# A two-layer decoder trunk: the gate columns of the MLP's up-projection by seven block products in every group

## The chip, the cores and the metric

One core of a Trainium2 chip runs the kernel as one program. TensorE (PE) multiplies matrices and writes its results to PSUM; its weight loads (PEld) overlap its matmuls. VectorE (DVE) and ScalarE (ACT) do elementwise work on SBUF and PSUM, GpSimd (POOL) a little of it on SBUF, and SyncE (SP) issues most DMAs. The metric is device time in microseconds; smaller is better.

## The reference

The input x is 512 tokens of 1024 features in f32. Two layers follow each other. Each is a mixer with an output projection (layer 0: sliding-window attention and a short convolution; layer 1: chunked gated linear attention, GLA), then a gated MLP, then a gated embedding. Every part adds to x. The MLP is what the change touches:

```python
def _rms_norm(x, gain):
    y = x * rsqrt(mean(x * x, axis=-1) + 1e-6)
    return y * gain

def _conv_ffn(h, w_up, conv_w, conv_b, w_down):       # h = _rms_norm(x, ffn_norm)
    u = causal_depthwise_conv(h @ w_up, conv_w) + conv_b       # 1024 -> 5632, width 3 along the tokens
    gate, up = split(u, 2, axis=-1)                            # 2816 each
    return (gelu(gate) * up) @ w_down                          # 2816 -> 1024
```

## The kernel before

**Layout and precision.** Activations lie transposed: x is eight tiles `xT[m]` of 128 features x 512 tokens. Every f32 operand is split into two parts of type fp32r, high and low (`split`, L97, for activations; `cut`, L119, and `cut_blocks`, L803, for weights): ACT copies the high part and DVE subtracts it from the operand to get the low one. A product is then three matmuls, high x high, high x low, low x high (`mm3`, L154; L863 to L865 for the block products). All of it fits into SBUF; weights come in loads of 1 MB by SP into two buffers `raw`, and their split parts go into three buffers `wh` and three `wl` of 1024 columns.

**Order.** The code is a straight program. A scheduler orders each engine's instructions by their place in the program and by when it expects them to be ready; each engine then runs its list strictly in that order. Inside `manual_schedule` TensorE's order is the program's own. A tile with a tag takes the next free buffer of that tag, and waits until one is free. The tags that matter here: `a0`, `a1`, `b0`, `b1` (eight tiles of 128x512 each), `four` (seven of 128x2048), `zt` (two), `z` (three), and in a small pool `sq` (two), `R` (two) and `acc` (one). PSUM has four banks `ps` and four `pa`.

**The norm.** In the output projection (`project`, L350) two blocks of output features at a time are multiplied: 8 input blocks x 3 matmuls of 512 columns for each. When a block is done, `residual` (L377) adds it to `xT[m]` (L379), and `advance` (L259) splits `xT[m]` times the gain (L105, L106) and sums the squares into `acc` (L270, L271). `end_norm` (L318) sums `acc` over the features with eight small matmuls (L324) and makes 1/rms of each token on DVE (L167) and POOL (L168); `spread` (L331) turns that into R, a tile that has each token's factor in every partition, with two matmuls (L345). The factor may be applied after a product, since it belongs to a token.

**The up-projection** (`ffn`, L894) has eleven groups d of two gate columns (128 features each) and two value columns. Groups 0 to 3 are plain: four columns of 24 matmuls with x that lacks R, and `taps` (L906) multiplies each result by R (L916) before the convolution (L917 on ACT, two L919 on DVE). While groups 0 and 1 run, `sums` (L775) makes x with gain and R (L782) and four sums and differences of its blocks and token halves, and splits them; in group 3 `normed` (L992) splits x with R again. Groups 4 to 10 (`SEVEN = (4, 11)`, L32) take their two gate columns from seven products of blocks instead of eight, the scheme of Winograd and Strassen: the weights' even and odd input blocks by two columns, x's even and odd blocks by two token halves. `seven` (L848) is a generator whose products run between the two value columns; `seven_forms` (L817) makes the weight blocks: plain, t13, t2, and later `last`. TensorE's order in such a group is: second value column, blocks 0 to 5 (`begin`, L1012); block product 1 of x's plain even blocks; the rest of that value column; product 2 with the sums s1; two products; half of the first value column; one product; the other half; two products. Results come out of `seven` without a product with R, since x has it; the second gate column needs one sum with the part `more` (L911).

**After the groups** the products gate x value are split for the down-projection (`split_acts`, L959, and `split_blocks`, L967) and `down` (L1099) works through a written plan of steps: rows B (f = 0 to 7), A (8 to 13), and C (14 to 21), C by seven block products for four or three of the four pairs of output blocks. In layer 1, `blocks` (L282) prepares the last norm's input, also by sums.

**The end of layer 1's mixer:** `gate` and `gated` (L1567, L1573) make the GLA's eight output blocks; the split results lie in tiles of the mixer's own pool until the projection has read them.

Of the kernel before, what the change touches and what calls it, by code (L numbers as in the profile page):

```python
# [9 lines left out]
F32 = mybir.dt.float32  # L10
# [21 lines left out]
SEVEN = (4, 11)  # L32
# [25 lines left out]
class Kernel:  # L58
# [223 lines left out]
    def blocks(self, m, gain, scratch):  # L282
# [4 lines left out]
        tags = ("a0", "a1") if m < 4 else ("b0", "b1")  # L287
# [62 lines left out]
    def project(self, load, ks, n_out, done, first=()):  # L350


        nk = len(ks)
        for m2 in range(0, n_out, 2):
            pss = [self.ps(), self.ps()]
            lead = [k0 for k0 in first if m2 == 0]
            k0s = lead + [k0 for k0 in range(0, nk, 8) if k0 not in lead]
            for k0 in k0s:
                kn = min(8, nk - k0)
                with self.tc.high_priority(offset=300 if lead else 0):  # L360
                    raw = self.raw(kn, 2 * P)
                    load(raw, k0, slice(m2 * P, (m2 + 2) * P))
                    w = self.cut(raw, "b")
                for c in range(2):
                    for k in range(kn):
                        self.mm3(
                            pss[c], w(k, c * P, (c + 1) * P), ks[k0 + k],
                            start=k0 == k0s[0] and k == 0, stop=k0 == k0s[-1] and k == kn - 1,
                        )
            for c in range(2):  # L370
                done(m2 + c, pss[c])

    def rows(self, w2d):
        wv = w2d.rearrange("(k p) n -> p k n", p=P)
        return lambda raw, k0, cols: self.nc.sync.dma_start(raw, wv[:, k0 : k0 + raw.shape[1], cols])

    def residual(self, gain):  # L377
        def done(m, ps):
            self.nc.vector.tensor_tensor(self.xT[m], self.xT[m], ps, ALU.add)  # L379
            self.advance(m, gain)  # L380

        return done
# [57 lines left out]
    def mixer0(self):  # L440
        nc, a, tc = self.nc, self.a, self.tc
        with tc.tile_pool(name="m0", bufs=1) as mp:
# [317 lines left out]
            self.begin_norm(("a0", "a1"))  # L760

            def load(raw, k0, cols):
                w = a["hy_w_out"][0]
                for g in range(2):
                    nc.sync.dma_start(
                        raw[64 * g : 64 * g + 64, :4, :],
                        w[256 * g : 256 * g + 256, cols].rearrange("(j p) n -> p j n", p=64),
                    )
                nc.sync.dma_start(raw[:, 4:, :], w[512:, cols].rearrange("(k p) n -> p k n", p=P))

            self.project(load, ya + yc, ND, self.residual(self.g_ffn[0]))
            self.end_norm()


    def sums(self, j, gain, R, scratch):  # L775


        nc = self.nc
        H = S // 2
        for u in range(2):  # L780
            m = 2 * j + u
            nc.vector.scalar_tensor_tensor(  # L782
                out=scratch[:, u], in0=self.xT[m], scalar=gain[:, m : m + 1], in1=R, op0=ALU.mult, op1=ALU.mult
            )
        e, o, s12, s34 = (scratch[:, u] for u in range(4))
        out = []
        nc.vector.tensor_tensor(s12[:, :H], e[:, H:], o[:, H:], ALU.add)
        nc.vector.tensor_tensor(s12[:, H:], s12[:, :H], e[:, :H], ALU.subtract)
        nc.vector.tensor_tensor(s34[:, :H], e[:, :H], e[:, H:], ALU.subtract)
        nc.vector.tensor_tensor(s34[:, H:], o[:, :H], s12[:, H:], ALU.subtract)  # L790
        for x in (s12, s34):
            hl = self.pair(self.fp, "b0", "b1")
            self.split(hl, x)
            for c in (slice(0, H), slice(H, S)):
                out.append((hl[0][:, c], hl[1][:, c]))
        return out
# [97 lines left out]
    def ffn(self, i, next_gain):  # L894
        nc, a, tc = self.nc, self.a, self.tc
        xg, R = self.xg, None
        gain = self.g_ffn[i]
        wu = a["ffn_w_up"][i].rearrange("(k p) n -> p k n", p=P)
        w0, w1, w2, bb = self.fcv
        with tc.tile_pool(name=f"ffn{i}", bufs=1) as fp:  # L900
            forms, kept, acts = [], [], [None] * NF
# [4 lines left out]
            def taps(y, ps, f, more=None, normed=True):  # L906
                z = ps
                if more is not None:
                    z = fp.tile([P, S + 2], F32, tag="z", name=self.nm("z"), bufs=3)[:, :S]
# [4 lines left out]
                elif not normed:  # L914
                    z = fp.tile([P, S + 2], F32, tag="z", name=self.nm("z"), bufs=3)[:, :S]
                    nc.vector.tensor_tensor(z, ps, R, ALU.mult)  # L916
# [7 lines left out]
            def columns(w, c, bank):  # L924
                ps = bank()
                for k in range(ND):
                    self.mm3(ps, w(k, c * P, (c + 1) * P), xg[k], start=k == 0, stop=k == ND - 1)
                return ps

            def loaded(d):  # L930
                out = [self.raw(ND, 256) for _ in range(2)]
                for raw, cols in zip(out, (gates(d), values(d))):
                    nc.sync.dma_start(raw, wu[:, :, cols])
                return out
# [1034 lines left out]
```

## Time and profile before

| What | Value |
|---|---|
| median of 3 runs | 1234.95 us (1234.46 to 1235.18) |
| the profiled execution, its own time | 1235.43 us |
| span of its profile | 1233.7 us |
| DMA traffic | 117.56 MB, mean 95 GB/s |
| output projection of layer 0 on TensorE | 140.6 to 184.3 us |
| plain groups 0 to 3 of layer 0 | 184.3 to 272.8 us |
| block groups 4 to 10 of layer 0 | 272.8 to 420.0 us |
| down-projection of layer 0 | 420.0 to 541.8 us |

The profile is one execution, recorded by the hardware; its times are counted from the span's start. A row of the page's groups gives line, engine, operation, output and inputs with their shapes, the count, then busy us and mean ns of one, then the idle time of the engine just before them and who ended it. A row of the timeline gives start, duration and the same names, and in brackets the idle time before it. "Busy" for TensorE counts a matmul to its modelled end, so consecutive matmuls overlap; the distance between two starts is what one costs.

### The profile page before, as it was taken

How to read it: one execution, taken by the hardware profiler on the slowest of the kernel's cores; microseconds unless marked ns; L12 is line 12 of the kernel's file. 1: busy time of each engine (PE TensorE's matmuls, PEld its weight loads, DVE VectorE, ACT ScalarE, POOL GpSimd, SP SyncE). 2: the span in 40 equal slices, each digit the busy share in tenths (PEclk: the TensorE clock that was granted, in tenths of full speed). 3: DMA queues.
4: the chain of work that ended last, by engine and by line, in shares of the span. 5: the costliest groups of instructions: out<-in, count | busy, mean ns of one | idle time of the engine just before them, and what ended most of it. 6: DMA issues, size and time to landing. Idle time of an engine off the chain costs nothing.

```text
span 1233.7 us, 16975 instructions
## 1 busy us (share of the span) xinstructions
PE 1222.7 (99%) x6740; PEld 1045.2 (85%) x6740; DVE 920.2 (75%) x1449; ACT 640.7 (52%) x1036; POOL 43.6 (4%) x64
## 2 busy tenths in 40 slices
PE   9999999999999999999999999999999999999998
PEld 8877788889999889888987888888889989889887
DVE  6886556987788986746679875558977779977595
ACT  7466434555556744534563554435455556645374
POOL 2500000000000000000100000000000000000000
PEclk9999999999999999999999999999999999999999
DMA  6221332323223333222322222322322322422501
GB/s 216 87 87 48 87 102 74 103 69 112 94 96 110 120 103 95 94 87 91 112 91 68 69 70 69 103 93 86 103 101 80 118 88 95 145 86 95 195 2 69
DMA packets 111060, 117.56 MB, mean 95 GB/s; under 512 B 2777, under 2 KB 106259, under 8 KB 110981
## 3 DMA queue, kind: packets, MB, share of 16 engines
q1 hardware_dynamic: 109616, 115.35, 28.7%
q8 instruction: 53, 0.87, 0.3%
q0 software_dynamic: 560, 0.42, 0.2%
q10 hardware_dynamic: 804, 0.70, 0.2%
q14 instruction: 27, 0.21, 0.1%
HBM read 114.37 MB, written 2.10 MB: 94 GB/s over the span
## 4 chain that ended last, share of the span: by engine, by line
PE 86%; DVE 9%; ACT 2%; issue 2%; POOL 1%; DMA 0%; ACTq 0%; DVEq 0%; POOLq 0%
PE ps L158 16%; PE ps L159 16%; PE ps L160 16%; PE pa L159 5%; PE pa L158 5%; PE pa L160 5%; PE ps L863 4%; PE ps L865 4%; PE ps L864 4%; PE pa L865 2%; PE pa L864 2%; PE pa L863 2%; DVE wl L139 1%; PE ps L1382 1%; PE ps L1381 1%
## 5 line engine op out<-in xcount | busy, mean ns | idle before, releaser
L138 ACT ACTIVATE wh<-raw 128x1024 fp32r<-128x1024 f32 (+4 forms) x170 | 169.4, 999 | 225.3 <-PE ps L159 168.0
L139 DVE TENSOR_TENSOR wl<-raw,wh 128x1024 fp32r<-128x1024 f32 (+4 forms) x170 | 195.1, 1149 | 95.1 <-ACT wh L138 94.8
L158 PE MATMUL ps<-a,wh 128*128 128x512 f32 x416 | 162.7, 391 | 0.0
L159 PE MATMUL ps<-a,wh 128*128 128x512 f32 x416 | 162.3, 390 | 0.0
L160 PE MATMUL ps<-a,wl 128*128 128x512 f32 x416 | 162.1, 390 | 0.0
L158 PE MATMUL ps<-b,wh 128*128 128x512 f32 x320 | 126.5, 396 | 0.6 <-ACT b L102 0.5
L160 PE MATMUL ps<-b,wl 128*128 128x512 f32 x320 | 125.7, 393 | 0.0
L159 PE MATMUL ps<-b,wh 128*128 128x512 f32 x320 | 125.2, 392 | 0.0
L811 ACT ACTIVATE wh<-raw 128x1024 fp32r<-128x1024 f32 x54 | 57.1, 1057 | 69.2 <-DVE raw L836 30.0
L158 PEld LDWEIGHTS ps<-a,wh 128*128 128x128 f32 x416 | 78.1, 188 | 16.6 <-issue 0.7
L159 PEld LDWEIGHTS ps<-a,wh 128*128 128x128 f32 x416 | 78.2, 188 | 16.4 <-issue 0.3
L160 PEld LDWEIGHTS ps<-a,wl 128*128 128x128 f32 x416 | 78.1, 188 | 16.3
L158 PE MATMUL pa<-a,wh 128*128 128x512 f32 x224 | 87.8, 392 | 0.0
L159 PE MATMUL pa<-a,wh 128*128 128x512 f32 x224 | 87.8, 392 | 0.0
L160 PE MATMUL pa<-a,wl 128*128 128x512 f32 x224 | 87.1, 389 | 0.0
L812 DVE TENSOR_TENSOR wl<-raw,wh 128x1024 fp32r<-128x1024 f32 x54 | 65.9, 1221 | 24.0 <-ACT wh L811 23.9
L158 PEld LDWEIGHTS ps<-b,wh 128*128 128x128 f32 x320 | 60.1, 188 | 13.9 <-ACT b L102 1.3
L919 DVE SCALAR_TENSOR_TENSOR zt<-z,vfa,zt 128x511 f32<-128x511 f32 (+1 forms) x92 | 67.2, 748 | 5.3 <-ACT zt L917 5.0
L160 PEld LDWEIGHTS ps<-b,wl 128*128 128x128 f32 x320 | 60.1, 188 | 12.8
L159 PEld LDWEIGHTS ps<-b,wh 128*128 128x128 f32 x320 | 60.2, 188 | 11.6
L160 PEld LDWEIGHTS pa<-a,wl 128*128 128x128 f32 x224 | 42.1, 188 | 9.2
L158 PEld LDWEIGHTS pa<-a,wh 128*128 128x128 f32 x224 | 42.3, 189 | 7.2
(460 smaller groups left out, 2942.4 us busy)
## 6 DMA issues: line engine op xcount, KB each, us to landing
raw<-in_ffn_w_up_dram SPq DMA_DIRECT2D x44, 1024.0 KB, 5.0
raw<-in_ffn_w_down_dram SPq DMA_DIRECT2D x13, 1024.0 KB, 5.1
raw<-in_hy_w_in_dram SPq DMA_DIRECT2D x8, 1024.0 KB, 5.0
raw<-in_gla_w_in_dram SPq DMA_DIRECT2D x8, 1024.0 KB, 5.2
raw<-in_ffn_w_down_dram SPq DMA_DIRECT2D x8, 768.0 KB, 4.6
raw<-in_ple_w_gate_dram SPq DMA_DIRECT2D x6, 1024.0 KB, 5.1
raw<-in_gla_w_out_dram SPq DMA_DIRECT2D x4, 1024.0 KB, 4.9
zt<-in_ffn_w_down_dram SPq DMA_DIRECT2D x6, 512.0 KB, 3.6
```

Of the source, the lines that this page charges most:

```text
L138: nc.scalar.activation(hv, v, AF.Copy)
L139: nc.vector.tensor_tensor(lv, v, hv.bitcast(F32), ALU.subtract)
L158: mm(out, lh, rh, start=start, stop=False, **kw)
L159: mm(out, lh, rl, start=False, stop=False, **kw)
L160: mm(out, ll, rh, start=False, stop=stop, **kw)
L811: nc.scalar.activation(h, src, AF.Copy)
L812: nc.vector.tensor_tensor(l, src, h.bitcast(F32), ALU.subtract)
L863: mm(out, wh, xh, start=first and j == 0, stop=False, **kw)
L864: mm(out, wh, xl, start=False, stop=False, **kw)
L865: mm(out, wl, xh, start=False, stop=j == ND // 2 - 1, **kw)
L919: nc.vector.scalar_tensor_tensor(out=y[:, tap:], in0=z[:, : S - tap], scalar=w[:, f : f + 1], in1=y[:, tap:], op0=ALU.mult, op1=ALU.add,)
L1381: mm(o, lh, rl, start=False, stop=False, **kw)
```

## The change

All eleven groups of both layers become block groups, and x enters them with its gain but without R.

- `sums`, `normed`, `residual` and the plain groups go. The projection now belongs to the MLP: the mixers return a function, and `ffn` calls it with `done`, which adds the residual and calls the new `operand(m)`. It copies `xT[m]` times the gain on ACT, splits the copy, and at each odd m makes and splits the four sums of that pair; then the square is summed. The sums' parts lie in four `four` buffers.
- `project` calls `then` ahead of the last two residuals; that is `prepare(0)`, which loads and cuts the weights of group 0.
- Group 0 contains `end_norm` after the first half of its first value column and `spread` after the second half.
- `taps` multiplies every result by R, the second gate column after its sum with `more`.
- `place` keeps the products of groups 0 to 3 in single tiles; `split_one` splits f = 0 to 5 in groups 4 to 9 and f = 6, 7 in the last; the double splits of f = 8, 10, 12 come after the groups, and the plan of `down` begins with B instead of A.
- The tags `a0`, `a1` and `b0`, `b1` change roles in layer 1 (`mine`, `other`), and the GLA's split results go to `a1`, `a0` and `R`, since the mixer's pool is closed before the projection.

```diff
-SEVEN = (4, 11)
-    def project(self, load, ks, n_out, done, first=()):
+    def project(self, load, ks, done, then):
+        for m2 in range(0, ND, 2):
             pss = [self.ps(), self.ps()]
+            raw = self.raw(ND, 2 * P)
+            load(raw, slice(m2 * P, (m2 + 2) * P))
+            w = self.cut(raw, "b")
+            for c in range(2):
+                for k in range(ND):
+                    self.mm3(pss[c], w(k, c * P, (c + 1) * P), ks[k], start=k == 0, stop=k == ND - 1)
+            if m2 + 2 == ND:
+                then()
             for c in range(2):
                 done(m2 + c, pss[c])
...
+    def operand(self, m, gain, tags):
+        nc, fp = self.nc, self.mlp
         H = S // 2
+        if m % 2 == 0:
+            self.scratch = self.four(fp, F32)
+        x = self.scratch[:, m % 2]
+        nc.scalar.activation(x, self.xT[m], AF.Copy, scale=gain[:, m : m + 1])
+        self.xg.append(self.pair(self.fp, *tags))
+        self.split(self.xg[m], x)
+        if m % 2:
+            e, o, s12, s34 = (self.scratch[:, u] for u in range(4))
+            nc.vector.tensor_tensor(s12[:, :H], e[:, H:], o[:, H:], ALU.add)
+            nc.vector.tensor_tensor(s12[:, H:], s12[:, :H], e[:, :H], ALU.subtract)
+            out = self.four(fp)
+            self.split((out[:, 0], out[:, 1]), s12)
+            nc.vector.tensor_tensor(s34[:, :H], e[:, :H], e[:, H:], ALU.subtract)
+            nc.vector.tensor_tensor(s34[:, H:], o[:, :H], s12[:, H:], ALU.subtract)
+            self.split((out[:, 2], out[:, 3]), s34)
+            self.forms.append([(out[:, q, c], out[:, q + 1, c]) for q in (0, 2) for c in (slice(0, H), slice(H, S))])
+        self.squares(m)
...
+        mine, other = (("a0", "a1"), ("b0", "b1"))[:: 1 - 2 * i]
...
-            def taps(y, ps, f, more=None, normed=True):
-                z = ps
-                if more is not None:
-                    z = fp.tile([P, S + 2], F32, tag="z", name=self.nm("z"), bufs=3)[:, :S]
+            def taps(y, ps, f, more=None):
+                z = fp.tile([P, S + 2], F32, tag="z", name=self.nm("z"), bufs=3)[:, :S]
+                if more is None:
+                    nc.vector.tensor_tensor(z, ps, R, ALU.mult)
+                else:
...
-                elif not normed:
-                    z = fp.tile([P, S + 2], F32, tag="z", name=self.nm("z"), bufs=3)[:, :S]
-                    nc.vector.tensor_tensor(z, ps, R, ALU.mult)
+                    nc.vector.tensor_tensor(z, z, R, ALU.mult)
...
+            def split_one(f):
+                tag = other[1 if f < 4 else 0]
+                h = self.fp.tile([P, S], F32R, tag=tag, name=self.nm("uh"))
+                pool, tag = (self.fp, tag) if f < 7 else (self.sp, "R")
+                acts[f] = h, pool.tile([P, S], F32R, tag=tag, name=self.nm("ul"))
+                self.split(acts[f], kept[f])
...
             def split_acts():
-                for f in (8, 10, 12):
-                    split_pair(f)
-                split_kept(0)
-                split_kept(1)
+                for f in (6, 7):
+                    split_one(f)
...
+            self.begin_norm(mine)
+            self.forms = []
+            xg = self.xg
+            ready = []
+            def done(m, ps):
+                nc.vector.tensor_tensor(self.xT[m], self.xT[m], ps, ALU.add)
+                self.operand(m, gain, mine)
+            project(done, lambda: ready.extend(prepare(0)))
+            steps, w1c, w0c = ready
+            with tc.manual_schedule(engines={ET.PE}):
+                late = begin(0, steps, w1c)
+                for d in range(groups):
+                    g, y = both(), both()
+                    next(steps)
+                    V0 = self.pa()
+                    value(w0c, V0, 0, ND // 2)
+                    if d == 0:
+                        self.end_norm()
+                    next(steps)
+                    value(w0c, V0, ND // 2, ND)
+                    if d == 0:
+                        R = self.spread()
+                    X, Y, more = next(steps)
+                    rest = late
+                    if d + 1 < groups:
+                        steps, w1c, w0c = prepare(d + 1)
+                        late = begin(d + 1, steps, w1c)
+                    else:
+                        split_acts()
+                    rest(y)
+                    taps(y[:, 0], V0, NF + 2 * d)
+                    taps(g[:, 0], X, 2 * d)
+                    taps(g[:, 1], Y, 2 * d + 1, more)
+                    nc.scalar.activation(g, g, AF.Gelu)
+                    place(d, g, y)
+                    if 4 <= d < groups - 1:
+                        split_one(d - 4)
...
+            for f in (8, 10, 12):
+                split_pair(f)
             self.down(i, acts, down_forms, both, work, finish)
...
-        plan = [(0, "A", 0, 3), (0, "A", 3, 6), (0, "B", 0, 4), (0, "B", 4, 8)]
+        plan = [(0, "B", 0, 4), (0, "B", 4, 8), (0, "A", 0, 3), (0, "A", 3, 6)]
...
             def gated(m):
-                if m < NT:
-                    hl = self.pair(mp, f"lah{m}", f"lal{m}")
-                else:
-                    hl = tuple(mp.tile([P, S], F32R, tag="F", name=self.nm("y"), bufs=8) for _ in range(2))
                 nc.vector.tensor_tensor(gs[m], gs[m], oT[m], ALU.mult)
+                pool, tag = (self.fp, "a0") if m + 1 < 2 * GH else (self.sp, "R")
+                hl = (
+                    self.fp.tile([P, S], F32R, tag="a1", name=self.nm("yh")),
+                    pool.tile([P, S], F32R, tag=tag, name=self.nm("yl")),
+                )
...
     def run(self):
         self.setup()
-        self.mixer0()
-        self.ffn(0, self.g_ple[0])
+        self.ffn(0, self.mixer0(), self.g_ple[0])
         self.ple0(self.g_mix[1])
-        self.mixer1()
-        self.ffn(1, self.g_ple[1])
+        self.ffn(1, self.mixer1(), self.g_ple[1])
```

More of the change, by code (lines that the diff above doesn't have):

```diff
@@ L759, in mixer0 @@
             conv_out(1)
[L760 to L771, printed above, removed]
```

221 lines of the change are left out of this document (61 added, 160 removed).

## The prediction

> **What bounds the kernel now.** I read the page's first lines, then stages (stretches of the span), then single instructions.
>
> ```profile
> span 1233.7 us, 16975 instructions
> PE 1222.7 (99%) x6740; PEld 1045.2 (85%) x6740; DVE 920.2 (75%) x1449; ACT 640.7 (52%) x1036; POOL 43.6 (4%) x64
> PE 86%; DVE 9%; ACT 2%; issue 2%; POOL 1%; DMA 0%; ACTq 0%; DVEq 0%; POOLq 0%
> ```
>
> TensorE is busy 99% of the span and is 86% of the chain that ended last. So an edit is worth what it takes from TensorE's own work, less the waits it puts in front of TensorE. Matmuls overlap, so I price one by the distance between starts, not by its "busy" time. First the timeline of TensorE (start, duration), then the stretches: the plain groups of layer 0, its seven block groups, those of layer 1, and two single block groups (columns: length, busy us and instruction count of each engine, granted clock, DMA share, GB/s).
>
> ```profile
> 297.23 0.39 PE L158 MATMUL pa<-a,wh 128*128 128x512 f32 x1
> 297.45 0.39 PE L159 MATMUL pa<-a,wh 128*128 128x512 f32 x1
> ...
> 298.38 0.28 PE L864 MATMUL pa<-a,wh 128*128 128x256 f32 x1
> 298.50 0.28 PE L865 MATMUL pa<-a,wl 128*128 128x256 f32 x1
> ```
>
> ```profile
> 196.63:272.79 76.16, 76.16 (x338) 63.06 (x337) 67.29 (x98) 39.81 (x53) 0.00 (x0) 1.00 0.27 87
> 272.79:420.03 147.24, 147.24 (x925) 133.52 (x924) 120.11 (x151) 85.76 (x125) 0.00 (x0) 1.00 0.30 99
> 908.85:1056.03 147.18, 147.18 (x925) 133.46 (x924) 120.06 (x151) 85.74 (x125) 0.00 (x0) 1.00 0.30 101
> 340.00:361.04 21.04, 21.04 (x134) 19.08 (x133) 16.37 (x21) 11.61 (x17) 0.00 (x0) 1.00 0.30 100
> 1018.00:1039.10 21.10, 21.10 (x134) 19.10 (x133) 19.73 (x24) 14.45 (x20) 0.00 (x0) 1.00 0.30 100
> ```
>
> The counts include one or two matmuls that straddle an edge. The plain stretch holds 336 starts: 76.16/336 = 0.2267 us for 512 columns. A plain group has 4 columns x 8 blocks x 3 = 96 of them, 21.76 us. A block group has 84 of 256 columns, 0.12 us apart (298.38 to 298.50), and 48 of 512; seven take 147.24 us, so one takes **21.03 us**, and 147.18/7 = 21.03 in layer 1. In these stretches TensorE never idles, and the granted clock is 1.00.
>
> **The change, part by part.**
>
> *Matmuls.* Four plain groups per layer become block groups: 8 x (21.76 - 21.03) = **-5.8 us**. The eight sums of the norm (L324) and the two matmuls that spread R (L345) only move. TensorE gets no other work and loses none. One rule speaks of this price. The Trainium skill, "TensorE: Matmul & The Clock Gate", section "Back-to-back issue gap", gives N/2.4 + 2.5 ns for N columns, 216 and 109 ns; by it the sum would be -9.5 us. The starts above are 227 and 120 ns apart, so the measurement decides; what it would bring is the third rival.
>
> *DVE and ACT in the groups.* x no longer carries R, so all four results of a group are multiplied by it:
>
> ```profile
> L916 DVE TENSOR_TENSOR z<-ps,R 128x512 f32<-128x512 f32 x32 | 21.7, 690 | 7.6 <-PE ps L160 7.5
> L139 DVE TENSOR_TENSOR wl<-raw,wh 128x1024 fp32r<-128x1024 f32 x135 | 165.1, 1224 | 83.9 <-ACT wh L138 83.7
> L835 DVE TENSOR_TENSOR raw<-raw 128x512 f32<-128x512 f32 x18 | 12.3, 683 | 0.0
> L782 DVE SCALAR_TENSOR_TENSOR four<-xT,vec,R 128x512 f32<-128x512 f32 x16 | 11.8, 750 | 0.0
> L106 DVE SCALAR_TENSOR_TENSOR a<-xT,vec,a 128x512 fp32r<-128x512 f32 x24 | 17.8, 746 | 0.0
> L103 DVE TENSOR_TENSOR a<-four,a 128x512 fp32r<-128x512 f32 x28 | 18.2, 687 | 0.0
> L102 ACT ACTIVATE a<-four 128x512 fp32r<-128x512 f32 x28 | 16.9, 627 | 9.0 <-DVE four L976 4.8 <-DVE four L977 3.9
> ```
>
> Four at 0.69 us add 2.8 us of DVE to each of the 14 old block groups, and the early splits of the products another 0.69 in groups 4 to 9: 16.4 + 2.8 + 0.7 = 19.9 us of 21.03. Each of the 8 new block groups also takes 1.5 more weight subtractions (1.8), four block sums like L835 (2.7) and the sum with `more` (0.7): 5.3 us. Per layer the norm's products (8 of L782), the second split of x (8 of L103) and the dearer form of the first (0.746 against 0.687) go: -12 us. Net (14 x 2.8 + 8 x 5.3) - 24 = +58 us, DVE near 978 us, 79% of the span. TensorE hides all of it: the last row of the stretches is a group with 19.73 us of DVE that TensorE ran through without idling. Without that cover DVE's excess over 21.03 us would count in full, in 22 groups. ACT goes to at most 14.45 + 1 us a group. Cost taken: 0.
>
> *Splits for the down-projection.* Six of the eight single splits of f = 0 to 7 move into groups 4 to 9. Two of the three double splits (f = 8, 10, 12) that ran earlier come behind the last group's taps, because x's sums hold four of the seven `four` buffers until TensorE has read them. From about 411 us on, where DVE's queue at the end of layer 0's groups begins, that is -6 x 0.69 + 2 x 1.22 + 4 x 0.69 (the last group's products with R) = +1 us.
>
> ```profile
> 418.91 2.49 DVE L103 TENSOR_TENSOR b<-four,b 128x512 fp32r<-128x512 f32 x4
> ...
> 428.47 0.42 DVE L975 TENSOR_TENSOR four<-four 128x256 f32<-128x256 f32 x1
> ...
> 449.50 1.29 DVE L103 TENSOR_TENSOR a<-zt,a 128x512 fp32r<-128x512 f32 x2
> ```
>
> ```profile
> 454.06 0.28 PE L863 MATMUL pa<-four,wh 128*128 128x256 f32 x1
> ```
>
> The last of the queue ends at 450.8; TensorE first reads those halves in its second block product, at 456.9 (454.06, 12 matmuls of 0.12 and 6 of 0.23). Six us of cover against +1: cost 0. The order B before A gives the three doubles 48 matmuls, 10.9 us; worth 0.
>
> *The seam between projection and group 0*, twice. Let E be the end of the projection. Before, group 0 reads x's eighth block after 21 matmuls and nothing else. After, the sequence is 18 matmuls, a block product, 6 matmuls, then a product that reads the sums of the last pair at E + 4.1 + 1.4 + 1.4 = E + 6.9. What must be done by then, from rows like these (residual, old split, then the norm's chain):
>
> ```profile
> 184.29 0.39 PE L158 MATMUL ps<-a,wh 128*128 128x512 f32 x1
> 184.49 0.69 DVE L379 TENSOR_TENSOR xT<-xT,ps 128x512 f32<-128x512 f32 x1 [2.08 <-PE ps L160]
> 185.35 1.23 DVE L139 TENSOR_TENSOR wl<-raw,wh 128x1024 fp32r<-128x1024 f32 x1 [0.18 <-ACT wh L138]
> 185.23 0.71 ACT L105 ACTIVATE a<-xT,vec 128x512 fp32r<-128x512 f32 x1
> 187.91 1.04 PE L324 MATMUL pa<-ones,acc 128*128 128x1 f32 x8
> 188.99 0.16 DVE L167 TENSOR_SCALAR rs<-pa 128x4 f32<-128x4 f32 x1 [1.15 <-PE pa L324]
> 188.81 0.48 PE L159 MATMUL ps<-a,wh 128*128 128x512 f32 x1
> 190.63 0.68 DVE L341 TENSOR_TENSOR dg<-cf,rhi 128x512 fp32r<-128x512 f32 x1
> 196.17 0.39 PE L345 MATMUL pa<-dg,ones_r 128*128 128x512 f32 x1
> ```
>
> E was 184.29, where group 0's first matmul starts. Residual 0.2 + 0.69, scaled copy 0.71, two half sums of 0.42, split 0.63 + 0.69: 3.8 us, 4.2 with the hops. Ahead in the queues stand the t13 split (ACT 1.06, DVE 1.22, released at E when its weight buffer comes free) and x's own split (0.69): up to 3.0. So 4.2 to 7.2 against 6.9. I take 0.3 us of waiting per seam; bounds 0 and 1.5 (if L843 and the t2 split stand ahead too).
>
> Behind it, two buffers are shared. `sq` has two, and the t2 weights hold both until product five, E + 11.2; the last squares and sums (1.3 us per block, two blocks overlapped: 2.0) may then start, and the norm's eight sums stand at E + 13.9. Cost 0, bound 1. From the end of those sums to the first spread matmul TensorE used to have 7.4 us (188.81 to 196.17), now a block product and twelve matmuls, 1.43 + 2.75 = 4.2; the chain took 2.5 (188.81 to 190.63 + 0.68). What queues behind a late spread matmul is TensorE itself, and behind R all taps of group 0. Cost 0, bound 1.7 if DVE and ACT make each hop wait. The projection's own DVE load, per pair of blocks 2 residuals, 2 + 2 splits, 2 norm sums, 4 half sums and 2 weight subtractions (8 x 0.69 + 4 x 0.42 + 2 x 1.22 = 9.6 us), lies under 48 matmuls, 10.9 us. The GLA gates now share eight `a0` buffers with their split results; at most eight are live, and gate 7 waits for gate 6's split (five steps of 0.63 to 0.69, 3.3 us, against 24 matmuls, 5.4 us). Cost 0.
>
> DMAs: the same 44 loads of 1 MB on SP's queue; group 0's two are issued ahead of the last residuals. Sum: -5.8 + 2 x 0.3 = **-5.2 us**. The profiled execution took 1235.43 us, its span 1233.7 and 1.7 around it; it lies 0.5 above the median, 1234.95. So 1230.2 there, and **1229.8** as a median.
>
> **The rivals.**
>
> *Slower: the weight chain in every group.* The chain from one group's last weight split to the next group's first:
>
> ```profile
> 345.80 1.06 ACT L811 ACTIVATE wh<-raw 128x1024 fp32r<-128x1024 f32 x1 [1.00 <-PE ps L864]
> 346.89 1.23 DVE L812 TENSOR_TENSOR wl<-raw,wh 128x1024 fp32r<-128x1024 f32 x1 [1.08 <-ACT wh L811]
> 353.05 1.06 ACT L138 ACTIVATE wh<-raw 128x1024 fp32r<-128x1024 f32 x1 [1.15 <-DMA raw<-in_ffn_w_up_dram]
> 354.15 1.23 DVE L139 TENSOR_TENSOR wl<-raw,wh 128x1024 fp32r<-128x1024 f32 x1 [2.51 <-ACT wh L138]
> 356.91 0.40 PE L158 MATMUL pa<-a,wh 128*128 128x512 f32 x1
> ```
>
> TensorE frees a buffer (345.7), ACT and DVE cut the last weights, the raw buffer comes free (348.1), a load follows, and its cut ends at 355.4, 1.5 us before TensorE needs it. DVE's idle 1.08 and 2.51 before the two subtractions is where the four products will go. If each waits for one tap (0.75), 1.5 us is just used up; if the program order sets two or three taps ahead of either, it is not. The price is the excess times 20 group boundaries: from 0.29 us each the gain is gone, and 0.7 us each gives 1229.8 + 14 = 1244. For it: DVE near 95% in groups 4 to 9. Against: the 19.73 us group kept TensorE fed, and weights are emitted before taps. The Trainium skill, same page, section "Architectural detail: the array is 16× 32×32, not 1× 128×128", says ACT and DVE are strict FIFO; by it a cut behind a waiting tap waits too, and no row here shows one overtaking. Chance 0.17.
>
> *Same: the seams take it back.* All bounds together, 2 x (1.5 + 1 + 1.7) = 8.4 us, would give 1237.5; half of them 1233.3. About 0.2% (2.5 us) is what a measurement of this kernel can tell from no change. Chance 0.13 for 1232.5 to 1237.4.
>
> *Faster still: cheaper block products.* If the added matmuls cost half of 0.227 each, a group would take 84 x 0.1135 + 48 x 0.229 = 20.5 us and the result would be near 1225.5. Fourteen measured groups speak against it: 0.02.
>
> **How the numbers follow.** Forecast 0.68 (1229.1 without any seam wait to 1232.4). Faster: 0.68 + 0.02 = 0.70; same 0.13; slower 0.17. The range 1228.7 to 1237.5 holds forecast and seam rival, 0.81; the slower rival is what is left out.
>
> **What would show it.** Eleven block groups per layer of 21.0 us each, x1452 matmuls in 231.4 us; no group boundary with an idle TensorE; the seam's first block product of the sums starting 6.9 to 7.2 us after E; spread 19 us after E. Wrong would be: a regular wait of TensorE on L139 or L812 at the boundaries (slower rival), a wait on the sums, `sq` or `dg` once per layer (seams), or a pitch other than 227 and 120 ns.

## The result, and the profile after

| Kernel | median | range | ratio to before, 95% interval |
|---|---|---|---|
| before | 1234.88 us | 1234.13 to 1235.36 (7 runs) | |
| changed | 1230.35 us | 1229.36 to 1231.84 (7 runs) | 0.9965 [0.9953, 0.9977] |

The change saves 4.5 us, 0.35%. The profiled execution took 1231.84 us, the slowest of the seven; its page begins:

```profile
span 1230.1 us, 17710 instructions
PE 1218.1 (99%) x7028; PEld 1053.8 (86%) x7028; DVE 969.7 (79%) x1537; ACT 665.7 (54%) x1084; POOL 43.7 (4%) x64
PE 79%; DVE 13%; ACT 3%; issue 2%; DMA 1%; POOL 1%; ACTq 0%; DVEq 0%; POOLq 0%
```

TensorE is as full as before, though it issues 288 more, shorter matmuls. DVE rises by 49.5 us (58 in the prediction) and takes 13% of the chain instead of 9%: something now waits for it. The stretches show where: first the eleven groups of each layer, then two groups of layer 0.

```profile
184.12:418.44 234.32, 233.74 (x1463) 211.17 (x1462) 206.84 (x278) 133.47 (x192) 1.04 (x1) 1.00 0.30 98
818.72:1052.43 233.71, 233.46 (x1463) 211.24 (x1462) 206.84 (x278) 133.60 (x192) 1.01 (x1) 1.00 0.30 99
248.57:270.76 22.19, 21.62 (x134) 19.05 (x133) 20.61 (x28) 13.59 (x20) 0.00 (x0) 1.00 0.29 96
270.76:291.80 21.04, 21.04 (x134) 19.08 (x133) 19.67 (x29) 12.55 (x19) 0.00 (x0) 1.00 0.31 100
```

A group without a wait takes 21.04 us, as in the kernel before; group 0 takes 22.36, because it holds the norm's sums and the spread. Eleven of them would make 232.76 us. Layer 0 takes 1.56 more, layer 1 0.95 more. From the projection's end to the down-projection's start layer 0 went from 235.74 us (184.29 to 420.03) to 234.32; without waits it would be 232.76. Everything outside the up-projection kept its length within 0.2 us.

The timeline of TensorE and DVE shows both the seam, which is in order, and the group that is not:

```profile
184.12 0.39 PE L157 MATMUL pa<-a,wh 128*128 128x512 f32 x1
...
190.19 1.29 DVE L102 TENSOR_TENSOR four<-four,four 128x512 fp32r<-128x512 f32 x2 [0.24 <-ACT four L101]
...
191.02 0.28 PE L845 MATMUL pa<-four,wh 128*128 128x256 f32 x1
...
198.09 0.95 PE L322 MATMUL pa<-ones,acc 128*128 128x1 f32 x8
...
248.04 1.23 DVE L138 TENSOR_TENSOR wl<-raw,wh 128x1024 fp32r<-128x1024 f32 x1 [0.85 <-ACT wh L137]
...
249.32 0.50 PE L159 MATMUL pa<-a,wl 128*128 128x512 f32 x1
...
257.79 1.22 DVE L138 TENSOR_TENSOR wl<-raw,wh 128x1024 fp32r<-128x1024 f32 x1
258.92 0.69 DVE L794 TENSOR_TENSOR t<-raw,t 128x512 fp32r<-128x512 f32 x1
...
259.66 0.39 PE L847 MATMUL ps<-four,t 128*128 128x256 f32 x1 [0.45 <-DVE t L794]
```

Seam: group 0 starts at 184.12, and the first product of the sums at 191.02, 6.90 us later and without idling. The first of the two splits, which it needs, ends near 190.9: the seam has about 0.1 us to spare. Group 3, which starts at 248.57, loses time in two places. At its start TensorE needs the low part of the second value column, w1, and its cut (L138) ends at 249.27, 0.70 us into the group: this costs 0.4 us. Later TensorE stands still before L847, for the low part of the t2 weights, which ends on DVE at 259.61: this costs 0.7 us. Ahead of it in DVE's list is the cut of the other value column, w0 (L138, 1.22 us). In the changed kernel four groups of each layer have w0's cut ahead of t2's, the others behind; the scheduler set this order once, when the program was built.

### The profile page after: what moved, and what is told of

Same layout as the page of the kernel before. It is cut to its first block, busy times and chain, and to the rows that moved or that the text cites. A ratio compares the mean times of both kernels' runs of the same rounds, so it can differ in the third digit from the quotient of the medians.

```text
span 1230.1 us, 17710 instructions
## 1 busy us (share of the span) xinstructions
PE 1218.1 (99%) x7028; PEld 1053.8 (86%) x7028; DVE 969.7 (79%) x1537; ACT 665.7 (54%) x1084; POOL 43.7 (4%) x64
## 4 chain that ended last, share of the span: by engine, by line
PE 79%; DVE 13%; ACT 3%; issue 2%; DMA 1%; POOL 1%; ACTq 0%; DVEq 0%; POOLq 0%
PE ps L157 12%; PE ps L158 11%; PE ps L159 11%; PE pa L158 6%; PE pa L157 6%; PE pa L159 6%; PE ps L847 5%; PE ps L845 5%; PE ps L846 5%; PE pa L847 2%; PE pa L846 2%; PE pa L845 2%; DVE wl L138 2%; DVE zt L905 1%; DMA raw<-in_ffn_w_up_dram 1%
## 5 line engine op out<-in xcount | busy, mean ns | idle before, releaser
L138 DVE TENSOR_TENSOR wl<-raw,wh 128x1024 fp32r<-128x1024 f32 (+4 forms) x154 | 175.3, 1139 | 50.6 <-ACT wh L137 48.6
L905 DVE SCALAR_TENSOR_TENSOR zt<-z,vfa,zt 128x510 f32<-128x510 f32 (+1 forms) x176 | 131.2, 747 | 9.6 <-ACT zt L903 8.9
L903 ACT ACTIVATE zt<-z,vfb 128x512 f32<-128x512 f32 x88 | 70.6, 809 | 16.4 <-DVE z L896 4.9
L157 PE MATMUL ps<-b,wh 128*128 128x512 f32 x192 | 76.2, 398 | 0.7 <-ACT b L101 0.5
L158 PE MATMUL ps<-b,wh 128*128 128x512 f32 x192 | 75.1, 392 | 0.0
L157 PE MATMUL pa<-b,wh 128*128 128x512 f32 x176 | 69.0, 392 | 0.0
L158 PE MATMUL pa<-b,wh 128*128 128x512 f32 x176 | 69.0, 392 | 0.0
L159 PE MATMUL pa<-b,wl 128*128 128x512 f32 x176 | 68.5, 389 | 0.0
L847 PE MATMUL ps<-four,wl 128*128 128x256 f32 x232 | 65.7, 283 | 0.0
L846 PE MATMUL ps<-four,wh 128*128 128x256 f32 x232 | 65.6, 283 | 0.0
L845 PE MATMUL ps<-four,wh 128*128 128x256 f32 x232 | 65.6, 283 | 0.0
L157 PE MATMUL ps<-a,wh 128*128 128x512 f32 x160 | 63.1, 394 | 0.0
L158 PE MATMUL ps<-a,wh 128*128 128x512 f32 x160 | 62.5, 391 | 0.0
L159 PE MATMUL ps<-a,wl 128*128 128x512 f32 x160 | 62.4, 390 | 0.0
L157 PE MATMUL ps<-uh,wh 128*128 128x512 f32 x128 | 50.3, 393 | 0.0
```

Of the source, the lines that this page charges most:

```text
L138: nc.vector.tensor_tensor(lv, v, hv.bitcast(F32), ALU.subtract)
L157: mm(out, lh, rh, start=start, stop=False, **kw)
L158: mm(out, lh, rl, start=False, stop=False, **kw)
L159: mm(out, ll, rh, start=False, stop=stop, **kw)
L845: mm(out, wh, xh, start=first and j == 0, stop=False, **kw)
L846: mm(out, wh, xl, start=False, stop=False, **kw)
```

## The experiments

The first theory, **order**: the waits come from these four groups. Rivals: **DVE is too full** (20.6 of 21.0 us), and **late loads**. In layer 0, the load behind w1's late cut in group 3 landed 7.1 us after its issue, where the median is 5.0. The table gives each kernel's time, and beside it the length of both up-projections in its profile (group 0's first matmul to the first one of the down-projection); without waits that is 465.5 us.

| Run | median (range) us | ratio to before [95%] | both up-projections |
|---|---|---|---|
| e1 changed kernel again | 1230.21 (1229.96 to 1230.35) | 0.9962 [0.9949, 0.9974] | 467.0 |
| e2 t2 ahead of w0 | 1231.68 (1230.25 to 1232.69) | 0.9973 [0.9962, 0.9984] | 468.8 |
| e3 value load first | 1228.79 (1228.53 to 1229.01) | 0.9950 [0.9938, 0.9963] | 465.5 |
| e4 no products with R | 1228.94 (1228.35 to 1230.51) | 0.9953 [0.9941, 0.9966] | 465.8 |
| e5 before, one more block group | 1235.71 (1234.58 to 1236.72) | 1.0006 [0.9998, 1.0015] | |
| e6 before, value load first | 1235.19 (1234.51 to 1235.35) | 1.0001 [0.9992, 1.0010] | |
| e7 w0 ahead of t2 | 1234.17 (1232.48 to 1235.51) | 0.9993 [0.9984, 1.0002] | 469.7 |
| e8 e7 and value load first | 1230.18 (1229.53 to 1230.55) | 0.9962 [0.9950, 0.9975] | 467.2 |
| e9 plain cut first | 1229.41 (1229.03 to 1229.93) | 0.9955 [0.9942, 0.9967] | 465.9 |
| e10 no prefetch ahead of residuals | 1230.82 (1229.95 to 1231.53) | 0.9965 [0.9952, 0.9977] | 468.3 |
| e11 A before B | 1243.46 (1242.36 to 1243.76) | 1.0066 [1.0054, 1.0079] | 466.9 |
| e12 e3 with R products twice | 1244.76 (1243.75 to 1245.73) | 1.0079 [1.0065, 1.0093] | 470.3 |

Except in e11 and e12, which disturb the down-projection too, the profiled execution's own time less its up-projections is 762.9 to 763.8 us in every version of the changed kernel: what moves the time is waiting in the up-projections.

**e1, the changed kernel again.**

> The changed kernel as it is, beside the three that follow. If the waits inside the block groups come from the fixed order of DVE's list (the order theory), a second execution shows them in the same groups: TensorE waits on the low part of the t2 weights (L794) in the groups that start near 248.6, 291.8, 355.2, 925.4 and 988.8 us, by 0.1 to 0.6 us each, and 1.0 to 2.0 us in all; time 1230.3, between 1229.4 and 1231.8. If they come from loads that happen to be late (the load theory), the groups with waits are others than before and their sum varies by over 1 us.

Waits stood in three of those four groups of each layer, 0.16 to 0.41 us each, and in no other, as the order theory said. But their sum fell from 2.5 to 1.4 us, and such a difference is what the load theory had named: most of it lies in group 3 of layer 0 (22.19 us, now 21.45), where the second load took 6.2 us instead of 7.1 and w1's cut was in time. In its timeline the chain that ends in t2 can be followed:

```profile
247.43 1.23 DVE L138 TENSOR_TENSOR wl<-raw,wh 128x1024 fp32r<-128x1024 f32 x1
248.57 1.22 DVE L794 TENSOR_TENSOR wl<-raw,wh 128x1024 fp32r<-128x1024 f32 x1
...
257.17 1.22 DVE L138 TENSOR_TENSOR wl<-raw,wh 128x1024 fp32r<-128x1024 f32 x1
258.31 0.69 DVE L794 TENSOR_TENSOR t<-raw,t 128x512 fp32r<-128x512 f32 x1
...
258.42 0.37 SPq L913 DMA_DIRECT2D raw<-in_ffn_w_up_dram  x1
...
261.42 0.37 SPq L913 DMA_DIRECT2D raw<-in_ffn_w_up_dram  x1
...
266.75 1.06 ACT L137 ACTIVATE wh<-raw 128x1024 fp32r<-128x1024 f32 x1 [0.64 <-DMA raw<-in_ffn_w_up_dram]
```

From w1's cut (247.43) to t2 (258.31) DVE does not pause once: cut of w1, cut of the plain blocks, differences, t13, difference, w0, t2, with the taps between. So t2 ends late when this stretch starts late. It starts when w1's cut can, and w1's weights come with the second of the two loads (issued 261.42, landed 266.73). The gate columns' load (258.42, landed 263.49) has by then been lying ready for 3 us, but its cut stands behind w1's in ACT's and DVE's lists.

**e2, t2 first in all groups.**

```diff
...
-                return self.seven(od, ws, xg, self.forms), w1, column(rv, 0)
+                with tc.issue_after(self.t2_cut[0]), tc.issue_after(self.t2_cut[1]):
+                    w0 = column(rv, 0)
+                return self.seven(od, ws, xg, self.forms), w1, w0
```

> Only the order is changed: the cut of the first value column's weights (w0) is queued behind the split of the t2 weights on ACT and on DVE in every group; in the kernel as changed four groups in each layer have it ahead. Order theory: t2's low part ends by 9.4 us after the start of its group everywhere (it is needed at 9.8), no TensorE wait on it is left, and 1.0 to 1.5 us are gained over the changed kernel: 1229.0 (1228.7 to 1229.5), with a narrower spread. Rival, DVE is simply too full (93% of a group): the work only changes places, the wait moves to the w0 column or to the last weights, and the time stays at 1230.0 to 1231. Load theory: unchanged as well, with waits of about 1 us behind a late load left.

Not faster: the order theory by itself fell. No wait on t2 is left, but others came at the group boundary, on w1's cut: they make five groups longer by 0.42 to 0.77 us, and a sixth by 0.17. The timeline of one (lines stand 2 lower here, L915 is the load, L849 the old L847):

```profile
934.62 0.37 SPq L915 DMA_DIRECT2D raw<-in_ffn_w_up_dram  x1
...
936.36 0.37 SPq L915 DMA_DIRECT2D raw<-in_ffn_w_up_dram  x1
...
943.78 1.06 ACT L137 ACTIVATE wh<-raw 128x1024 fp32r<-128x1024 f32 x1 [1.94 <-DMA raw<-in_ffn_w_up_dram]
...
944.88 1.23 DVE L138 TENSOR_TENSOR wl<-raw,wh 128x1024 fp32r<-128x1024 f32 x1 [0.98 <-ACT wh L137]
...
946.16 0.50 PE L159 MATMUL pa<-b,wl 128*128 128x512 f32 x1 [0.47 <-DVE wl L138]
```

w0's cut is what frees the buffer for the next group's first load. Cut later, it brings the first load to 1.7 us ahead of the second instead of 3.5 (the same pair in e1), and the second then took 7.4 us to land. The delay comes back one group later, in front of w1.

**e3, the value columns' load first.** Two lines: which buffer is filled first.

```diff
-                out = [self.raw(ND, 256) for _ in range(2)]
-                for raw, c0 in zip(out, (256 * d, DFF + 256 * d)):
+                out = [self.raw(ND, 256) for _ in range(2)][::-1]
+                for raw, c0 in zip(out[::-1], (DFF + 256 * d, 256 * d)):
```

> Only the order of the two loads of a group is changed: the value columns' weights, which are cut first, are issued ahead of the gate columns'. Their buffer comes free about 12 us earlier than the gate columns', so a late load has cover. It also puts the t2 split ahead of w0's cut in all groups of DVE's list. Order theory and load theory: no waits inside groups, 1229.0 (1228.5 to 1229.5). Rival, the third buffer of split weights: the w1 cut, ready earlier, takes the buffer that the last gate weights wait for, and waits on L794 appear at every boundary: 1232 to 1236. Rival, DVE too full: 1230 to 1231.

As the order and load theories expected; the rivals of the third weight buffer and of a full DVE fell. Its stretches (both up-projections, then one group):

```profile
184.08:416.84 232.76, 232.76 (x1463) 211.12 (x1462) 208.71 (x278) 132.86 (x192) 1.04 (x1) 1.00 0.30 99
816.66:1049.42 232.76, 232.76 (x1463) 211.12 (x1462) 208.77 (x278) 132.94 (x192) 1.01 (x1) 1.00 0.30 99
227.48:248.52 21.04, 21.04 (x134) 19.08 (x133) 20.45 (x30) 12.90 (x19) 0.00 (x0) 1.00 0.31 100
```

No wait is left in 22 groups, and DVE is busy 20.45 of 21.04 us in one of them. It isn't the load that hurts at this level. The timeline shows the stretch shifted:

```profile
255.73 0.69 DVE L794 TENSOR_TENSOR t<-raw,t 128x512 fp32r<-128x512 f32 x1
...
256.57 1.23 DVE L138 TENSOR_TENSOR wl<-raw,wh 128x1024 fp32r<-128x1024 f32 x1 [0.16 <-ACT wh L137]
...
257.83 0.37 SPq L913 DMA_DIRECT2D raw<-in_ffn_w_up_dram  x1
...
260.80 0.37 SPq L913 DMA_DIRECT2D raw<-in_ffn_w_up_dram  x1
...
264.02 1.06 ACT L137 ACTIVATE wh<-raw 128x1024 fp32r<-128x1024 f32 x1 [0.18 <-PE ps L846]
```

The loads leave 9.3 and 12.3 us into the group (e1: 9.7 and 12.7): the first buffer comes free 3 us earlier, not the 12 of the expectation. But the first load now carries the value columns: w1's cut starts at 264.02, 15.5 us into its group, instead of 18.1 (266.75, of a group that began at 248.69). From group 1 on, t2 ends 7.0 to 8.0 us into its group instead of up to 10.3.

**e4, no products with R.**

```diff
-                    nc.vector.tensor_tensor(z, ps, R, ALU.mult)
+                    z = ps
...
-                    nc.vector.tensor_tensor(z, z, R, ALU.mult)
```

> Leaves out the products with R in the up-projection (four per group, 88 in all, 61 us of DVE), so the result lacks the norm's factor there. DVE falls from 18.6-20.6 to about 16-18 us per group. Order theory and DVE-too-full: both expect the waits to go, 1228.9 (1228.5 to 1229.4); with waits left of more than 0.5 us in all, they come from loads and not from DVE. This is also what the most could be that DVE's load costs. If the time stays at 1230.3, DVE's load isn't the cause at all.

The waits go (0.3 us left). So a lighter DVE cures it, and so does e3 with the full load: what the products cost is their place in the stretch before t2, not their sum.

**e5 and e6, two controls on the kernel before.** e5 sets `SEVEN = (3, 11)`, e6 makes e3's edit in the old `loaded`.

> The kernel before with one more block group in each layer (groups 3 to 10 instead of 4 to 10) and nothing else of the change: the price of the matmuls by itself. By the pitch of 227 and 120 ns a block group takes 21.03 us and a plain one 21.76: -0.73 us twice, -1.5 in all, 1233.4 (1233.0 to 1234.2). By the rival of cheaper added matmuls -2.5, 1232.4; if the gain is lost in the groups -0.5 or less, 1234.4.

> The kernel before with the value columns' load ahead of the gate columns' in its seven block groups per layer. Load-chain theory (a group of the changed kernel waits because the load that is cut first is issued last, and its chain of load, w1 cut, plain cut, block differences, t13 and t2 ends where TensorE needs t2): before has no wait in these groups, so nothing changes, 1234.9 within 0.3. Rival (the order of the loads gains by itself, for instance by fewer conflicts): about -1 us here too.

e6 came out as the load-chain theory said: 0.3 us above before, no change. e5 missed: +0.8 instead of -1.5. Its eight block groups have the price that was expected, all but one in each layer, the second:

```profile
272.11:294.08 21.97, 21.59 (x135) 19.05 (x133) 16.65 (x21) 10.99 (x16) 0.00 (x0) 1.00 0.30 97
```

```profile
280.50 1.23 DVE L139 TENSOR_TENSOR wl<-raw,wh 128x1024 fp32r<-128x1024 f32 x1 [0.40 <-ACT wh L138]
...
282.24 0.68 DVE L812 TENSOR_TENSOR t<-raw,t 128x512 fp32r<-128x512 f32 x1
...
282.98 0.39 PE L865 MATMUL ps<-b,t 128*128 128x256 f32 x1 [0.34 <-DVE t L812]
```

It takes 21.97 us, 0.93 too much, in both layers, in a group where DVE is busy only 16.65 us. A third of it is lost at the group's start on w1's cut, whose load was issued 1.8 us after the other; the rest is t2 behind w0's cut again. This one group costs 1.9 us and the pitch brings 1.5; the 0.4 left over is half of the 0.8 measured. The other half doesn't show in the traces: the two profiled executions, 1235.71 and 1235.43 us, differ by only 0.3. The run shows that the wait doesn't need a full DVE.

**e7 and e8, w0 ahead of t2 in all groups**, with the old order of loads and with e3's:

```diff
...
-                ws = self.seven_forms(ev, od, rg)
-                return self.seven(od, ws, xg, self.forms), w1, column(rv, 0)
+                plain, t13 = self.first_forms(ev, od, rg), self.cut_blocks(ev)
+                w0 = column(rv, 0)
...
+                nc.vector.tensor_tensor(b11, b22, b11, ALU.subtract)
+                with tc.issue_after(self.last_cut[0]), tc.issue_after(self.last_cut[1]):
+                    t2 = self.cut_blocks(b11, False)
+                nc.vector.tensor_tensor(b21, b21, b11, ALU.subtract)
+                return self.seven(od, (plain, t13, t2), xg, self.forms), w1, w0
```

> The changed kernel, loads in their old order, with the opposite order of e2: the split of t2 stands behind the cut of w0 in all eleven groups of each layer, on ACT and DVE. w0's buffers come free at 8.2 us in a group at the earliest, so t2 ends at 9.9 or later against a need at 9.8. Load-chain theory: 1230.5 to 1233, with t2 at 9.9 to 10.6 and waits of 0 to 0.6 us per group, because the loads wait for the cuts either way. Order theory, as first held: 0.2 to 0.5 us in each of the 20 groups, 1233 to 1239.

> As e7, but with the value columns' load ahead of the gate columns'. Load-chain theory: the chain has 2.4 us of room, so t2 ends at 9.9 in nearly all groups, waits stay under 0.1 us each, 1229 to 1230. Order theory: as slow as e7, within 0.5 us.

e7 (1234.17) is above what the load chain gave and inside what the order theory gave; e8 (1230.18) is 4.0 us better than e7 and so no "as slow as e7". The two orders act together. With the gate load first, the three orders of t2 and w0 (t2 first, mixed, w0 first) give 1231.7, 1230.2 and 1234.2; with the value load first, t2 first gives 1228.8 and w0 first 1230.2. From these runs the need of t2 can be read: groups where it ended at 9.88 us took 21.03 us, at 9.99 21.15, at 10.24 21.39. Each 0.1 us past 9.88 costs 0.1 us.

**e9, the plain cut first.** Loads as in the changed kernel; the load that lands first is cut first.

```diff
-                w1 = column(rv, 1)
                 ev, od = self.by_parity(rg)
-                ws = self.seven_forms(ev, od, rg)
+                plain = self.first_forms(ev, od, rg)
+                w1 = column(rv, 1)
+                ws = plain, self.cut_blocks(ev), self.more_forms(ev, od)
```

> The changed kernel with the loads in their old order (gate columns first, value columns about 3 us later), but the cut of the gate columns' plain blocks and the block differences stand ahead of the cut of the value column w1 in the program, so that the load that lands first is cut first. Load-chain theory, made narrower: what costs is that ACT's and DVE's lists begin with the load that lands last, while the other lies ready for 3 us; then this gains as much as e3, 1228.8 (1228.5 to 1229.3), with t2 ending 7.5 to 9 us after the start of a group. Rival: it is the early value load itself that helps (w1's cut is the tight one, 1 us ahead of TensorE): then w1, now behind the plain cut, is late by 0 to 1 us at each of 20 boundaries, 1231 to 1245.

The narrower theory held in its mechanism: t2 ends 5.8 to 6.3 us into every group from the second on, even earlier than expected. The time, 1229.41, is 0.1 us above its range and 0.6 above e3. As in e3, t2 now stands ahead of w0's cut in all groups; e2 shows that this alone gains nothing. Of the rival a trace remains: w1's cut ends up to 0.44 us into a group, which costs 0.15 us twice and less than 0.04 elsewhere.

**e10 and e11, two other parts of the change undone.** e10 calls `then()` behind the residuals; e11 puts A first in the plan and the loads of `down`.

> The changed kernel with the preparation of group 0's weights placed behind the last two residuals of the projection instead of ahead of them (that part of the change undone). The loads start when their buffers come free, which doesn't change; only the cuts and the splits of x change places in ACT's and DVE's lists. Theory (the seam has room: t13 and the sums are needed 6.9 us after the projection's end): 0 to 0.7 us per seam, 1230.2 to 1231.6. Rival (the prefetch is what hides the seam): the cuts of group 0 come after the whole operand work, 3 to 5 us per seam, 1236 to 1240.

> The changed kernel with the down-projection's plan beginning with A (f = 8 to 13) instead of B (f = 0 to 7), that part undone. In the changed kernel the double splits of f = 10 and 12 end 5 and 8 us after the last group (DVE, 423.3 and 426.4 us against 417.8), behind that group's taps. A reads f = 10 after 2.7 us and f = 12 after 5.5 us: TensorE waits 2 to 5 us at the start of each down-projection, 1234 to 1240. Rival, the scheduler puts the double splits ahead of the taps and the waits move to the last group's products, which are needed 36 us later: 1230.2, unchanged.

e10: group 0 takes 22.4 us in both layers, as with the prefetch, so the seam doesn't need it. The 1.3 us by which its up-projections exceed e1's lie in groups 2 and 3 of layer 0, which take 21.40 and 22.40 us; the load that was late in the first profiled execution took 6.6 us here. e11 lost 13 us, more than expected. TensorE's and DVE's timeline, and the two stretches, one in each layer, in which the granted clock was low:

```profile
421.05 0.39 PE L157 MATMUL ps<-four,wh 128*128 128x512 f32 x1
...
423.86 1.22 DVE L102 TENSOR_TENSOR four<-four,four 128x1024 fp32r<-128x1024 f32 x1
...
425.13 0.79 PE L158 MATMUL ps<-four,wh 128*128 128x512 f32 x1 [3.69 <-DVE four L102]
425.72 0.63 PE L159 MATMUL ps<-four,wl 128*128 128x512 f32 x1
426.15 0.63 PE L157 MATMUL ps<-four,wh 128*128 128x512 f32 x1
...
430.42 0.45 PE L158 MATMUL ps<-four,wh 128*128 128x512 f32 x1
430.71 0.39 PE L159 MATMUL ps<-four,wl 128*128 128x512 f32 x1
...
1065.25 0.67 PE L158 MATMUL ps<-four,wh 128*128 128x512 f32 x1 [3.68 <-DVE four L102]
...
1068.70 0.45 PE L157 MATMUL ps<-four,wh 128*128 128x512 f32 x1
```

```profile
423.71:430.54 6.83, 5.41 (x13) 4.25 (x14) 6.83 (x8) 3.88 (x4) 0.00 (x0) 0.50 0.01 2
1065.41:1068.82 3.41, 3.41 (x9) 2.67 (x10) 3.41 (x5) 2.51 (x3) 0.00 (x0) 0.50 0.24 71
```

The wait for f = 10 (3.85 us beyond the usual pitch) is as expected. What I had not expected comes behind it: matmuls start 0.43 us apart instead of 0.23, and the granted clock is 0.50. The 12 matmuls from 425.13 to 430.42 take 5.29 us instead of 2.73. That adds 2.6 us, and makes 6.4. In layer 1 the wait is as long, but the clock is low for 3.4 us only: 8 matmuls, from 1065.25 to 1068.70, are slow, which adds 1.6 and makes 5.5. The two layers together are 11.9 of the 13.2 us lost against e1; 0.6 more is a wait of 0.3 us on a double split at the start of each down-projection.

**e12, DVE's load past a group's length** (e3 and a second `tensor_tensor(z, z, R, ALU.mult)` before the taps).

> e3 (value load first) with every product with R made twice (88 more DVE instructions at 0.60 us from start to start, 2.4 us per group, so the factor enters squared). It doses DVE's load past a group's length. DVE busy per group goes from 18.6-20.5 to 21.0-22.9 of 21.04 us; groups 2 to 5 exceed it by 1.0 to 1.9. Theory that the excess over 21.03 counts in full: 6 to 8 us per layer, 1241 to 1245. If the excess is pushed into lighter groups (buffers allow a delay), only the mean counts, 235 of 233 us per layer: 1231 to 1235. If DVE was already the limit in the changed kernel, 2.4 us x 22: 1280.

16.0 us slower than e3. The excess over 21.03 us that I had added up is 7 us per layer, 14 in all. Stretches of e12 (layer 0's groups together, two groups, the start of the down-projection), and TensorE's waits from 360 to 480 us:

```profile
184.03:418.75 234.72, 233.29 (x1464) 211.23 (x1462) 226.77 (x315) 131.16 (x190) 1.04 (x1) 1.00 0.30 98
248.47:269.51 21.04, 21.04 (x134) 19.08 (x133) 21.04 (x31) 11.81 (x17) 0.00 (x0) 1.00 0.31 101
374.71:397.70 22.99, 21.56 (x134) 19.19 (x133) 22.99 (x33) 13.60 (x20) 0.00 (x0) 1.00 0.28 92
418.75:470.00 51.25, 47.20 (x234) 39.09 (x233) 45.05 (x67) 26.21 (x37) 0.00 (x0) 1.00 0.35 115
```

```profile
PE ps L159 <- DVE wl L138: 1.5, 1, 1.5
PE pa L846 <- DVE four L102: 1.1, 1, 1.1
PE pa L845 <- ACT a L101: 1.1, 1, 1.1
PE pa L847 <- DVE wl L794: 1.0, 1, 1.0
```

DVE works through whole groups without a gap, and TensorE still runs on at 21.04 us in most of them: taps slip back from group to group. The bill comes in group 9 and in the down-projection's start. The changed kernel is well away from that cliff.

## Why the prediction was right, point by point

The forecast was 1229.8 us, the result 1230.35. The sum nearly held because two of its terms were off in opposite directions; to that extent it was luck.

- **Matmuls, -5.8 us: right.** e3 shows the change without any wait: 232.76 us per layer against 235.74 in layer 0 before, 1228.79 us, -6.1. The pitch of 227 and 120 ns stands; the 1463 matmuls of a stretch are the 1452 forecast (eleven groups of 132), the norm's ten and one at the edge. The rival of cheaper products fell.
- **Seams, 0.3 us each: too dear.** They cost nothing; the product of the sums starts 6.90 us after the projection's end (forecast 6.9 to 7.2), and the spread 19.0 us after it. The wait on the buffers `sq` and on R did not come either. e10 shows that the prefetch isn't the reason.
- **"TensorE hides all of it. Cost taken: 0" for DVE in the groups: this step failed**, by 1.4 us (e1) to 2.5 us (the first profiled execution, 0.4 of it at the boundary of group 3). I had set DVE's sum for a group, 19.9 us, against the group's length and against one group of 19.73 us that didn't wait. (That row, from 1018.00 on, straddles two groups; the one that starts at 1013.95 has 19.67.) The sum was about right (18.6 to 19.9 measured in groups 4 to 9 of layer 0, 20.6 in group 3) and the wrong thing to look at: e3 runs 20.45 us without a wait, and e5 loses 0.93 us at 16.65. What decides is when t2 ends, 9.88 us into a group at the latest.
- **The slower rival, the weight chain.** Its mechanism was real, its place and number mostly not. At the boundary, where I had looked for it, w1's cut now ends 0.04 to 0.85 us ahead of the group's start in e1's layer 0 from the third group on (0.52 to 1.54 before): tighter, but enough. It wasn't enough once in the first profiled execution, behind the late load: w1's cut ended 0.70 us into group 3 and cost 0.4 us. Otherwise the chain was too long at its other end, at t2, and in three groups of each layer, not at 20 boundaries. The rule of strict order that the prediction took from the Trainium skill, "TensorE: Matmul & The Clock Gate", section "Architectural detail: the array is 16× 32×32, not 1× 128×128", is borne out by e1 and e9. In e1 the plain cut, whose load had landed at 263.49, started on ACT at 267.71, behind w1's cut, which waited for its load until 266.75; in e9, where the list has the plain cut first, it started at 264.20.
- **The down-projection, 0: right** for the splits and the new order together. Down's start has no new wait, and e11 shows what the order B before A is there for: with A first, the splits that the change moved cost 13 us. So "worth 0" holds only as a part of the pair.
- **"DVE's excess over 21.03 us would count in full"**: e12 bears it out, 16.0 us for a forecast of 12 to 16, though most of it is paid after the groups.

Shown: the place of the waits, and that either the load order (e3), the cut order (e9) or a lighter DVE (e4) removes nearly all of them. Open: why the second load was so late in single cases (7.1 us in the first profiled execution, 6.2 in e1, 6.6 in e10, same place). Group 3 accounts for 0.7 of the 1.5 us between the first two of these executions; the rest of the changed kernel's scatter of 2.5 us isn't traced. Open too is half of e5's loss.

The best version is e3, 1228.79 us. Its slowest run (1229.01) is below the changed kernel's fastest (1229.36), though the intervals of the ratios overlap.

## What to carry to other kernels

When an engine in order stands between the loads and TensorE, don't compare its busy sum with the group's length; follow its list from the load that releases it to the operand with the earliest need, and count all that stands between. Issue first the load that is cut first, or cut first what lands first. And when a part of a change looks worth nothing, ask which other part would be late without it.

## What the runs showed of the hardware

- **A long wait is paid twice.** In e11 TensorE is without a matmul for 3.7 us once in each layer. The granted clock was then 0.50 for 6.8 us in layer 0, from 423.71 on, while TensorE still waited, and for 3.4 us in layer 1, from 1065.41 on: 0.43 us from start to start. In e12, waits up to 1.5 us left the clock at 1.00. The Trainium skill, "TensorE: Matmul & The Clock Gate", section "Part 1: The HAM clock gate", has the rule: about 3.4 us of idling bring the half clock, 427 ns per matmul of 512 columns, until about as long a busy time has passed. The trace agrees with the 427 ns, and in layer 1 with the length; in layer 0 the slow time was twice that, of which 5.3 us fell on matmuls.
- **Two loads of 1 MB issued close together: the second lands late.** Of 119 second loads of a group that were issued 2.9 to 4 us after the first, over all fourteen traces, 109 landed within 4.8 to 5.6 us; the seven issued under 2 us after it (five in e2, two in e5) took 6.1 to 7.4 us. In between, both occur, up to 7.1 us. (For about a quarter of the pairs the profile gives no landing.)
